# Wide gate and up products in four FFN parts, state space angle tables moved into the end of the second mix part, both score maps issued together

## The chip, the cores and the metric

The program runs on one core of one Trainium2 chip. The metric is the device time of one execution in microseconds (us). One execution was also profiled; all rows below are of that one.

## What is computed

The reference takes 256 tokens of width 1024 through three blocks. The first one has two layers; what matters of it:

```python
for l in range(DEPTH):                                   # 2 layers
    h = h + 0.5 * swiglu(rmsnorm(h, ffn1_norm[l]), ...)   # parts f10, f11
    u = rmsnorm(h, mix_norm[l])
    c_q, c_kv, k_rope, dq, dk, dv, p_in, z_gate = split(u @ w_in[l])
    # latent attention, differential attention (two softmax maps per head,
    # 8 heads), windowed pooling; each gated by sigmoid(z_gate) and projected
    h = h + merged @ w_out[l]                             # parts mx0, mx1
    h = h + 0.5 * swiglu(rmsnorm(h, ffn2_norm[l]), ...)   # parts f20, f21

swiglu(x) = (silu(x @ w_gate) * (x @ w_up)) @ w_down      # 1024 -> 2816 -> 1024
```

The second block (stick-breaking attention beside an S5 state space layer) and the third (gated linear attention) follow. For the S5 layer the kernel makes tables of sines and cosines of angles, from its parameters alone, some time before they are needed.

## The kernel before

**Numbers.** All products are float32 made of three matmuls on rounded parts: a weight tile `wh` (rounded) and `wl` (the rest), an activation tile hi and lo. `mm3` (L314) issues wh by hi, wh by lo, wl by hi into one accumulator: a *triple* (L317, L318, L319). Activations are held transposed, features on partitions and all 256 tokens (T) along the free axis, 8 chunks k for the width of 1024. Where tokens must stand on partitions (values, sigmoid gates), `tokens` multiplies the other way round, with 512 columns of the weight as the moving operand (L643 to L645).

**Weights.** `W()` (L299) takes the next weight piece, 128 x 1024, out of a raw buffer that SP's queue filled (two pieces a transfer, three buffers); ACT copies the rounded part `wh` (L311), DVE subtracts to get `wl` (L312). There are six wh/wl buffers: a piece takes the one of the piece six before it.

**FFN.** `ffn` (L532) runs over NF = 22 blocks f of 128 hidden features. For each: gate and up products by `project(f)` (two times 8 triples, gate and up being halves of one PSUM bank of tag a or b in turn), then the down products of block f-1 (8 triples into four banks of tag c, which stay open over the whole part), then the end of block f: DVE gate by the norm's row factor (L588), ACT silu (L589), POOL by half the row factor (L590), DVE by up (L591), `split` into hi on ACT (L339) and lo on DVE (L340). The result `hs[f]` is needed one block later, by down. Blocks 0 to 2 are projected early, while the norm's statistics are made. The last two blocks' down products stand at the end, bank by bank, so that the residual add of each bank can start.

**Mix.** `mix` (L717) makes latent attention, then differential attention in eight steps, one per head; `dscores` issues the score products of a head's two maps (32 rows of contraction each, one PSUM tile each) and their softmax. Between the steps stand fills for TensorE: the pooling windows (`window(g)`, on DVE), their products (`pooled(g)`, L848), value and gate projections and branch products. At the end of the part come the branch products with the differential output (`branch(1, g, ...)`, sinks L809 and L821 take them out of PSUM on ACT and DVE), the transposes of the differential output (`to_chunks`, L712; its scaling L933 on DVE), `turn(g)` (transposes of the merged output and its split, L339/L340), and the output projection (`out_steps`), whose results go to the next part's residual.

**S5 tables.** `s5_prep` (L959) returns a list of steps. `begin` makes step sizes and reduced angles with small operations on POOL, ACT and DVE that hand to one another (L979 to L991); eight `table` steps (two of 16 angle rows each) go DVE, POOL, DVE, POOL, POOL, DVE (L1001 to L1008); `sines` applies the sine on ACT; `begin_outs` to `direct` multiply out coefficient tables on POOL and DVE and transpose them. Part f21 takes one of these steps at the head of each block, f = 1 to 19.

**Order.** The program is written in the order of the parts. The tile framework then lists each engine's instructions by a scheduler that looks ahead; what an engine runs first is thus that list, and a wait holds all behind it on the same engine.

Of the kernel before, what the change touches and what calls it, by code (L numbers as in the profile page):

```python
# [238 lines left out]
class Kern:  # L239
# [75 lines left out]
    def mm3(self, ps, wh, wl, xh, xl, start, stop):  # L315
        mm = self.nc.tensor.matmul
        mm(ps, wh, xh, start=start, stop=False, skip_group_check=True)  # L317
        mm(ps, wh, xl, start=False, stop=False, skip_group_check=True)  # L318
        return mm(ps, wl, xh, start=False, stop=stop, skip_group_check=True)  # L319

    def proj(self, ps, w, xs, nk, off=0, m=P, stride=P):
        for k in range(nk):
            s = slice(off + k * stride, off + k * stride + m)
            last = self.mm3(ps, w[0][:, s], w[1][:, s], xs[0](k), xs[1](k), k == 0, k == nk - 1)
        return last

    def in_turn(self, pss, names, xs, starts):

        ws = [self.W(n) for n in names]
        for k in range(8):  # L330
            for ps, w, start in zip(pss, ws, starts):
                m = ps.shape[0]
                s = slice(k * m, k * m + m)
                self.mm3(ps, w[0][:, s], w[1][:, s], xs[0](k), xs[1](k), k == 0 and start, k == 7)
# [10 lines left out]
    def pair(self, n):  # L345

        s = [[self.slot(F32R) for _ in range((n + 3) // 4)] for _ in range(2)]
        return tuple((lambda k, q=q: q[k // 4][:, k % 4]) for q in s)
# [74 lines left out]
    def out_steps(self, tag, ks, ys, evac):  # L423
# [4 lines left out]
        def blk(w, k, d):  # L428
            self.mm3(acc[d // 2][:, (d % 2) * T:(d % 2) * T + T], w[0][:, d * P:(d + 1) * P],
                     w[1][:, d * P:(d + 1) * P], ys[0](ks[k]), ys[1](ks[k]),  # L430
# [101 lines left out]
    def ffn(self, part, l, h, extra=()):  # L532
# [6 lines left out]
        def down(f, d, w, hs):  # L539
            self.mm3(acc[d // 2][:, (d % 2) * T:(d % 2) * T + T], w[0][:, d * P:(d + 1) * P],  # L540
                     w[1][:, d * P:(d + 1) * P], hs[:, 0], hs[:, 1],
# [4 lines left out]
        def project(f, *ups):  # L546
            ups = ups or (0, 1)
            if f not in pgu:
# [8 lines left out]
            for k in range(8):  # L557
                for up, w in zip(ups, ws):
                    self.mm3(pgu[f][up], w[0][:, k * P:(k + 1) * P], w[1][:, k * P:(k + 1) * P],
                             xs[0](k), xs[1](k), k + up == 0, k == 7)  # L560

        for f in range(NF):
            if 0 < f <= len(extra):
                extra[f - 1]()
            if f == 0:
# [6 lines left out]
                with project(*todo.pop(0)):  # L572
                    stats(st[:, T:T + 2])
                project(*todo.pop(0))
                rb = self.rows(rc, st[:, 0:T])
                nc.scalar.activation(hrb, rb, AF.Copy, scale=0.5)
                project(*todo.pop(0))
            elif f == 1 and todo:
# [9 lines left out]
            nc.vector.tensor_tensor(gs, pg, rb, ALU.mult)  # L588
# [20 lines left out]
    def small_norm(self, cks, g, n):  # L609
# [18 lines left out]
        return (lambda k: hss[k][:, 0]), (lambda k: hss[k][:, 1])  # L628
# [88 lines left out]
    def mix(self, part, l, h):  # L717
# [143 lines left out]
        for f in more[1:] + gate(2, 0) + gate(2, 1) + branch(2, 0, yp) + branch(2, 1, yp) + \  # L861
# [32 lines left out]
        def dscores(hd):  # L894
# [3 lines left out]
            pp = []  # L898
            for m, rs in ((0, s0), (1, s1)):
# [752 lines left out]
```

## Time and profile before

| what | before |
|---|---|
| time, 3 runs | 1593.46, 1594.07 (median), 1594.55 us |
| the profiled execution | 1593.75 us |
| its span in the trace | 1592.0 us |
| TensorE busy | 1561.0 us, 98% of the span, 11662 matmuls |
| VectorE (DVE) busy | 1039.5 us, 65% |
| ScalarE (ACT) busy | 823.6 us, 52% |
| GpSimd (POOL) busy | 344.3 us, 22% |
| read from memory | 258.96 MB, 163 GB/s |

The time of an execution is its span plus some 1.8 us around it. A row of the timeline gives the start of an instruction, how long it took, engine, line, operation, output and inputs, and in brackets the idle time of the engine before it with what ended that. Matmuls overlap: how fast they follow one another is read from their starts, not from their lengths. A row with x4 stands for four instructions that follow one another, and its length is that of all four.

### The profile page before, as it was taken

The page shows a single profiled execution, that of the slowest core. Times are in us where ns is not written, and L with a number is a line of the kernel's source. Part 1 is how long each engine was busy: PE and PEld are TensorE (multiplying, and loading weights), DVE is VectorE, ACT ScalarE, POOL GpSimd, SP SyncE. Part 2 cuts the span into 40 slices and gives each one's busy share as a digit, 9 for nine tenths or more (in the row PEclk, how much of TensorE's full clock was granted, in tenths as well). Part 3 has the DMA queues.
Part 4 walks back from the last instruction along what each step waited for, and adds up shares of the span by engine and source line. Part 5 has one row for each costly group of instructions (what it writes and reads, how often), then busy time and mean ns, then how long its engine had stood idle before and what let it go on. Part 6 is the DMA issues. An engine that isn't in the chain of part 4 may idle for free.

```text
span 1592.0 us, 28666 instructions
## 1 busy us (share of the span) xinstructions
PE 1561.0 (98%) x11662; PEld 1451.4 (91%) x11662; DVE 1039.5 (65%) x1728; ACT 823.6 (52%) x1422; POOL 344.3 (22%) x414
## 2 busy tenths in 40 slices
PE   8999999999999999999999999999999999999998
PEld 8999998888999999999999878899899987899877
DVE  7655586575775557655576576776585787777743
ACT  6444455565454445444455556454444645566663
POOL 4111142001121112111132200244331321112232
PEclk9999999999999999999999999999999999999999
DMA  8555543344455554555544343554355443442430
GB/s 286 191 184 186 186 166 133 137 155 159 159 185 186 186 185 138 209 186 185 186 169 159 130 159 133 180 204 160 133 212 178 147 154 134 155 157 85 185 132 27
DMA packets 38451, 261.84 MB, mean 164 GB/s; under 512 B 4336, under 2 KB 5616, under 8 KB 7344
## 3 DMA queue, kind: packets, MB, share of 16 engines
q1 hardware_dynamic: 37440, 257.61, 45.0%
q0 software_dynamic: 736, 2.34, 0.5%
q8 instruction: 91, 1.49, 0.4%
q14 instruction: 40, 0.33, 0.1%
q10 hardware_dynamic: 144, 0.08, 0.0%
HBM read 258.96 MB, written 1.05 MB: 163 GB/s over the span
## 4 chain that ended last, share of the span: by engine, by line
PE 81%; DVE 8%; POOL 5%; ACT 3%; issue 3%; DMA 0%; SPq 0%; DVEq 0%; POOLq 0%; ACTq 0%
PE psa L318 7%; PE psa L317 7%; PE psa L319 7%; PE psc L318 6%; PE psc L319 6%; PE psc L317 6%; PE psb L317 5%; PE psb L318 5%; PE psb L319 5%; PE psa L643 5%; PE psa L645 5%; PE psa L644 5%; DVE wl L312 2%; ACT wh L311 1%; PE psb L643 1%
## 5 line engine op out<-in xcount | busy, mean ns | idle before, releaser
L312 DVE TENSOR_TENSOR wl<-raw,wh 128x1024 fp32r<-128x1024 f32 (+1 forms) x487 | 602.9, 1243 | 266.5 <-ACT wh L311 265.5
L311 ACT ACTIVATE wh<-raw 128x1024 fp32r<-128x1024 f32 (+1 forms) x487 | 507.8, 1050 | 417.9 <-PE psa L318 125.3
L317 PE MATMUL psa<-s,wh 128*128 128x256 f32 (+1 forms) x1224 | 349.3, 285 | 2.9 <-DVE s L1226 1.7
L318 PE MATMUL psa<-s,wh 128*128 128x256 f32 (+1 forms) x1224 | 348.4, 285 | 1.9 <-DVE s L343 1.5
L319 PE MATMUL psa<-s,wl 128*128 128x256 f32 (+1 forms) x1224 | 346.3, 283 | 0.2 <-DVE wl L312 0.2
L317 PEld LDWEIGHTS psa<-s,wh 128*128 128x128 f32 (+1 forms) x1224 | 233.7, 191 | 6.9 <-DVE s L1226 1.9
L318 PEld LDWEIGHTS psa<-s,wh 128*128 128x128 f32 (+1 forms) x1224 | 233.7, 191 | 6.1 <-DVE s L343 4.3
L590 POOL TENSOR_TENSOR t<-t,hrb 128x256 f32<-128x256 f32 x88 | 121.7, 1383 | 521.0 <-ACT t L589 521.0
L319 PEld LDWEIGHTS psa<-s,wl 128*128 128x128 f32 (+1 forms) x1224 | 233.8, 191 | 0.6 <-DVE wl L312 0.4
L319 PE MATMUL psb<-s,wl 128*128 128x256 f32 x752 | 212.9, 283 | 1.1 <-DVE wl L312 1.1
L317 PE MATMUL psb<-s,wh 128*128 128x256 f32 x752 | 213.6, 284 | 0.0
L318 PE MATMUL psb<-s,wh 128*128 128x256 f32 x752 | 212.8, 283 | 0.0
L317 PE MATMUL psc<-hs,wh 128*128 128x256 f32 x704 | 198.8, 285 | 4.5 <-ACT hs L339 4.5
L318 PE MATMUL psc<-hs,wh 128*128 128x256 f32 x704 | 200.3, 285 | 2.7 <-DVE hs L340 1.9
L319 PE MATMUL psc<-hs,wl 128*128 128x256 f32 x704 | 198.8, 283 | 0.0
L319 PEld LDWEIGHTS psb<-s,wl 128*128 128x128 f32 x752 | 144.3, 192 | 1.3 <-DVE wl L312 1.3
L317 PEld LDWEIGHTS psb<-s,wh 128*128 128x128 f32 x752 | 144.3, 192 | 0.5 <-ACT t L1335 0.3
L318 PEld LDWEIGHTS psb<-s,wh 128*128 128x128 f32 x752 | 144.4, 192 | 0.0
L317 PEld LDWEIGHTS psc<-hs,wh 128*128 128x128 f32 x704 | 134.3, 192 | 6.4 <-ACT hs L339 6.1
L318 PEld LDWEIGHTS psc<-hs,wh 128*128 128x128 f32 x704 | 135.0, 192 | 5.4 <-DVE hs L340 5.2
L643 PE MATMUL psa<-wh,s 128*128 128x512 f32 x336 | 137.5, 409 | 0.0
L319 PEld LDWEIGHTS psc<-hs,wl 128*128 128x128 f32 x704 | 135.1, 192 | 0.0
(390 smaller groups left out, 2514.6 us busy)
## 6 DMA issues: line engine op xcount, KB each, us to landing
raw<-in_w SPq DMA_DIRECT2D x242, 1024.0 KB, 4.8
s<-in_x SPq DMA_DIRECT2D x4, 256.0 KB, 5.4
raw<-in_w SPq DMA_DIRECT2D x4, 256.0 KB, 6.0
out<-t SPq DMA_DIRECT2D x8, 128.0 KB, 1.7
cst<-in_cst SPq DMA_DIRECT2D x1, 545.5 KB, 7.8
sq<-in_pw POOLq DMA_DIRECT2D x2, 256.0 KB, 3.7
s<-in_s5b POOLq DMA_DIRECT2D x1, 512.0 KB, 3.6
s<-in_s5c POOLq DMA_DIRECT2D x1, 512.0 KB, 3.7
```

The lines of the kernel that those rows point to most:

```text
L311: self.act = nc.scalar.activation(hi[:, s], src[:, s], AF.Copy)
L312: nc.vector.tensor_tensor(lo[:, s], src[:, s], hi[:, s].bitcast(F32), ALU.subtract)
L317: mm(ps, wh, xh, start=start, stop=False, skip_group_check=True)
L318: mm(ps, wh, xl, start=False, stop=False, skip_group_check=True)
L319: return mm(ps, wl, xh, start=False, stop=stop, skip_group_check=True)
L590: nc.gpsimd.tensor_tensor(sg, sg, hrb, ALU.mult)
L643: mm(ps[b], xs[0](k)[:, t], w[0][:, s], start=k == 0, stop=False, skip_group_check=True)
L644: mm(ps[b], xs[0](k)[:, t], w[1][:, s], start=False, stop=False, skip_group_check=True)
L645: mm(ps[b], xs[1](k)[:, t], w[0][:, s], start=False, stop=k == 2 * n - 1, skip_group_check=True)
```

## The change

1. `pair` now stores hi and lo of one chunk side by side, so that [hi | lo] is one operand of 512 columns. `mm3` and its callers take that pair; what they issue is as before.
2. A new function `wide` serves the gate and up products of blocks f = 3 to 21: in place of a triple it issues one matmul of wh by [hi | lo] (512 columns, into both halves of a bank) and one of wl by hi (256 columns, into the first half). Gate and up get a bank each, tags a and b. At the end of the block ACT copies the second half of each bank to a temporary and DVE adds the first half to it, for gate and for up (L611, L612); the rest of the chain (L613, L617, L618, L619, split L349 and L350) is as before.
3. The scores of a head's two maps are issued in turn: 128 columns of one and of the other, 256 columns of one and of the other. Both PSUM tiles are taken first.
4. `pooled(g)` stands one attention step later, two steps behind its window.
5. `begin` and the eight `table` steps are put in the second mix part's end, one behind each branch and output step; `sines`, cut in two, goes into block 0 of f21; the other S5 steps stand at f = 1 to 9 of f21.

```diff
-    def mm3(self, ps, wh, wl, xh, xl, start, stop):
+    def mm3(self, ps, wh, wl, x, start, stop):
...
+    def wide(self, ps, w, xs):
+
+        mm = self.nc.tensor.matmul
+        for k in range(8):
+            s = slice(k * P, k * P + P)
+            mm(ps, w[0][:, s], xs[2](k).rearrange("p a t -> p (a t)"), start=k == 0, stop=False,
+               skip_group_check=True)
+            last = mm(ps[:, 0:T], w[1][:, s], xs[0](k), start=False, stop=k == 7, skip_group_check=True)
+        return last
...
         def project(f, *ups):
             ups = ups or (0, 1)
+            if f > 2:
+                pgu[f] = self.psa("a"), self.psa("b")
+                for up in ups:
+                    last = self.wide(pgu[f][up], self.W(part + "gu"[up] + str(f)), xs)
+                return self.tc.issue_after(last.ins)
...
-            nc.vector.tensor_tensor(gs, pg, rb, ALU.mult)
+            if f > 2:
+                up = self.tmp()
+                for t, ps in ((gs, pg), (up, pu)):
+                    nc.scalar.activation(t, ps[:, T:2 * T], AF.Copy)
+                    nc.vector.tensor_tensor(t, ps[:, 0:T], t, ALU.add)
+                nc.vector.tensor_tensor(gs, gs, rb, ALU.mult)
+                pu = up
+            else:
+                nc.vector.tensor_tensor(gs, pg, rb, ALU.mult)
...
-            fills.append([lambda g=g: window(g)] if g == 0 else
-                         [lambda g=g: window(g), lambda g=g: pooled(g - 1)])
+            fills.append([lambda g=g: window(g)] if g < 2 else
+                         [lambda g=g: window(g), lambda g=g: pooled(g - 2)])
...
-        fills.append([more[0], lambda: pooled(3)])
+        fills.append([more[0], lambda: pooled(2)])
+        fills.append([more[1], lambda: pooled(3)])
...
-            pp = []
-            for m, rs in ((0, s0), (1, s1)):
-                i = 2 * hd + m
-                r = slice(32 * (i % 4), 32 * (i % 4) + 32)
-                ps = self.psa("b", 384)
-                self.qk(ps, dq[r, i // 4], dk[r, i // 4])
-                pp.append(self.softmax(ps, bias, [rs[:, hd:hd + 1], rs[:, 8 + hd:9 + hd]]))
+            pss = [self.psa("b", 384) for _ in range(2)]
+            rows = [slice(32 * (i % 4), 32 * (i % 4) + 32) for i in (2 * hd, 2 * hd + 1)]
+            for o, b, n in ((0, 0, P), (P, P, T)):
+                for r, ps in zip(rows, pss):
+                    nc.tensor.matmul(ps[:, o:o + n], dq[r, hd // 2, b:b + P], dk[r, hd // 2, 0:n],
+                                     start=True, stop=True)
...
         for g in range(2):
             for f in branch(1, g, yd, "ab"[g]):
                 f()
+                more()
...
+            prep = self.s5_prep() if l else ()
+            h = self.mix("mx%d" % l, l, h, prep[:9])
+            h = self.ffn("f2%d" % l, l, h, prep[11:], prep[9:11])
```

Where the instructions stand now. First ACT, in the end of the second mix part, around the two sinks of the last gate projection (`s<-psa,sm`: L809 before, L837 now; `sq` is the square sum of the differential output, `s5p` the S5 parameters, `vec` constants). Before:

```order
L921 ACTIVATE sq_11040<-psc_10354 128x512
L921 ACTIVATE sq_11043<-psc_10355 128x512
L311 ACTIVATE wh_11197<-raw_11195 128x1024
L809 ACTIVATE s_11084<-psa_10997,sm_9807 128x512
L809 ACTIVATE s_11084<-psa_10998,sm_9807 128x512
L311 ACTIVATE wh_11213<-raw_11195 128x1024
L311 ACTIVATE wh_11237<-raw_11235 128x1024
```

and with the change:

```order
L311 ACTIVATE wh_10628<-raw_10626 128x1024
L1020 ACTIVATE s5p_8620<-vec_86 128x16
L1023 ACTIVATE s5p_8620<-s5p_8620 128x16
L1024 ACTIVATE s5p_8620<-s5p_8620 128x16
L837 ACTIVATE s_10515<-psa_10428,sm_9238 128x512
L1030 ACTIVATE s5p_8620<-s5p_8620 128x16
L837 ACTIVATE s_10515<-psa_10429,sm_9238 128x512
L311 ACTIVATE wh_10665<-raw_10626 128x1024
L311 ACTIVATE wh_10703<-raw_10701 128x1024
```

Four operations of `begin` now stand between the weight copy and the two sinks, three ahead of the first and one between them.

Second DVE, a little later: the sinks of the branch products (L821 before, L849 now) and the scaling of the differential output (L933 before, L964 now; `t` are temporaries of the table steps). Before:

```order
L312 TENSOR_TENSOR wl_11214<-raw_11195,wh_11213 128x1024
L312 TENSOR_TENSOR wl_11238<-raw_11235,wh_11237 128x1024
L821 SCALAR_TENSOR_TENSOR s_10722<-s_10722,psa_11087 128x512
L821 SCALAR_TENSOR_TENSOR s_10722<-s_10722,psa_11088 128x512
L933 TENSOR_TENSOR s_11036<-psc_10354,sm_11038 128x512
L933 TENSOR_TENSOR s_11036<-psc_10355,sm_11038 128x512
```

and with the change:

```order
L312 TENSOR_TENSOR wl_10666<-raw_10626,wh_10665 128x1024
L1046 TENSOR_SCALAR t_10686<-t_10686 128x256
L1041 TENSOR_SCALAR t_10720<-cst_85,s5p_8620 128x128
L1040 TENSOR_SCALAR t_10754<-cst_85,s5p_8620 128x128
L1041 TENSOR_SCALAR t_10755<-cst_85,s5p_8620 128x128
L1043 TENSOR_SCALAR t_10721<-t_10721 128x256
L1040 TENSOR_SCALAR t_10754<-cst_85,s5p_8620 128x128
L312 TENSOR_TENSOR wl_10704<-raw_10701,wh_10703 128x1024
L849 SCALAR_TENSOR_TENSOR s_10153<-s_10153,psa_10518 128x512
L849 SCALAR_TENSOR_TENSOR s_10153<-s_10153,psa_10519 128x512
L964 TENSOR_TENSOR s_10467<-psc_9785,sm_10469 128x512
L964 TENSOR_TENSOR s_10467<-psc_9786,sm_10469 128x512
```

Between the weights' second parts and the sinks now stand six table operations, among them L1046 and L1043, each of which takes what POOL made of the operations before.

Third ACT at the end of an FFN part (f10), from the weight ahead of block 21's gate to the rounding of its result. Before:

```order
L311 ACTIVATE wh_2425<-raw_2419 128x1024
L311 ACTIVATE wh_2486<-raw_2484 128x1024
L589 ACTIVATE t_2266<-t_2265 128x256
L339 ACTIVATE hs_2272<-t_2267 128x256
L311 ACTIVATE wh_2520<-raw_2484 128x1024
```

and with the change:

```order
L611 ACTIVATE t_2070<-psa_2026 128x256
L311 ACTIVATE wh_2296<-raw_2294 128x1024
L611 ACTIVATE t_2073<-psb_2027 128x256
L617 ACTIVATE t_2071<-t_2070 128x256
L311 ACTIVATE wh_2330<-raw_2294 128x1024
L349 ACTIVATE hs_2082<-t_2072 128x256
```

The two copies of the second halves are new, and a weight copy of the next part stands between them, another one ahead of the rounding L349.

## Rows read from the trace of the kernel before

**Rows 1.** Page, part 1: busy time, share of the span and instructions of each engine.

```profile
PE 1561.0 (98%) x11662; PEld 1451.4 (91%) x11662; DVE 1039.5 (65%) x1728; ACT 823.6 (52%) x1422; POOL 344.3 (22%) x414
```

**Rows 2.** Timeline of PE in f10; 57 matmuls of 256 columns, first and last.

```profile
99.73 0.28 PE L319 MATMUL psa<-s,wl 128*128 128x256 f32 x1
...
106.45 0.28 PE L318 MATMUL psb<-s,wh 128*128 128x256 f32 x1
```

**Rows 3.** Timeline of PE in the first mix part; 24 matmuls of 512 columns, first and last.

```profile
389.65 0.39 PE L645 MATMUL psa<-wh,s 128*128 128x512 f32 x1
...
394.86 0.40 PE L645 MATMUL psb<-wh,s 128*128 128x512 f32 x1
```

**Rows 4.** Timeline of PE in the second mix part; 6 matmuls of 512 columns, first and last.

```profile
1005.00 0.40 PE L644 MATMUL psa<-wl,s 128*128 128x512 f32 x1
...
1006.17 0.39 PE L643 MATMUL psa<-wh,s 128*128 128x512 f32 x1
```

**Rows 5.** Timeline of PE, the scores of one head's two maps (two records a matmul).

```profile
346.23 0.50 PE L664 MATMUL psb<-s 32*128 32x128 f32 x4
346.55 0.60 PE L665 MATMUL psb<-s 32*128 32x256 f32 x4
```

**Rows 6.** Groups by line and form: pooling products; busy, mean ns | idle before, releaser.

```profile
L848 PE MATMUL psc<-t,sq 128*128 128x256 f32 x16 | 5.3, 411 | 3.1 <-DVE t L842 3.1
```

**Rows 7.** Groups by line and form: weights' two parts and the end of an FFN block.

```profile
L312 DVE TENSOR_TENSOR wl<-raw,wh 128x1024 fp32r<-128x1024 f32 x482 | 599.9, 1250 | 265.0 <-ACT wh L311 264.0
L311 ACT ACTIVATE wh<-raw 128x1024 fp32r<-128x1024 f32 x482 | 505.0, 1055 | 415.8 <-PE psa L318 125.3 <-PE psb L318 91.0 <-PE psa L645 72.5
L590 POOL TENSOR_TENSOR t<-t,hrb 128x256 f32<-128x256 f32 x88 | 121.7, 1383 | 521.0 <-ACT t L589 521.0
L588 DVE TENSOR_TENSOR t<-psb,rb 128x256 f32<-128x256 f32 x44 | 18.6, 423 | 18.1 <-PE psb L319 18.1
L339 ACT ACTIVATE s<-psa 128x256 fp32r<-128x256 f32 x16 | 5.4, 378 | 3.7 <-DVE s L340 3.7
```

**Rows 8.** Timeline of PE at the end of f10, first products of the last hidden block.

```profile
197.81 0.38 PE L317 MATMUL psc<-hs,wh 128*128 128x256 f32 x1 [0.25 <-ACT hs L339]
198.27 0.39 PE L318 MATMUL psc<-hs,wh 128*128 128x256 f32 x1
```

**Rows 9.** Timeline of PE: starts of like matmuls in f20 (two) and f21 (three).

```profile
437.29 0.28 PE L317 MATMUL psa<-s,wh 128*128 128x256 f32 x1
468.76 0.28 PE L317 MATMUL psa<-s,wh 128*128 128x256 f32 x1
...
1054.96 0.28 PE L317 MATMUL psa<-s,wh 128*128 128x256 f32 x1
1087.99 0.28 PE L317 MATMUL psa<-s,wh 128*128 128x256 f32 x1
...
1182.73 0.28 PE L317 MATMUL psa<-s,wh 128*128 128x256 f32 x1
```

**Rows 10.** Groups by line and form: the last step of a table but one, on DVE.

```profile
L1007 DVE TENSOR_SCALAR t<-t 128x256 f32<-128x256 f32 x8 | 2.9, 360 | 13.0 <-POOL t L1006 13.0
```

**Rows 11.** Timeline of all engines in the second mix part's end.

```profile
1002.66 2.93 POOL L927 TENSOR_TENSOR sm<-sm,cst 128x16 f32<-128x16 f32 x1 [110.49 <-DVE sm L926]
1003.92 1.37 ACT L809 ACTIVATE s<-psa,sm 128x512 f32<-128x512 f32 x2 [0.98 <-PE psa L645]
1004.67 0.50 PE L643 MATMUL psa<-wh,s 128*128 128x512 f32 x1
1011.17 1.28 DVE L933 TENSOR_TENSOR s<-psc,sm 128x512 f32<-128x512 f32 x2
1012.76 0.49 PE L712 MATMUL psc<-cst,s 128*128 128x128 f32 x3
1029.44 0.75 DVE L340 TENSOR_TENSOR s<-psa,s 128x256 fp32r<-128x256 f32 x2
1029.91 0.39 PE L318 MATMUL psc<-s,wh 128*128 128x256 f32 x1 [0.25 <-DVE s L340]
```

More of the change, by code (lines that the diff above doesn't have):

```diff
@@ L333, in in_turn @@
                 s = slice(k * m, k * m + m)
-                self.mm3(ps, w[0][:, s], w[1][:, s], xs[0](k), xs[1](k), k == 0 and start, k == 7)
+                self.mm3(ps, w[0][:, s], w[1][:, s], xs[2](k), k == 0 and start, k == 7)
     def split(self, hi, lo, src, scale=None):
@@ L345, in pair @@
     def pair(self, n):
-        s = [[self.slot(F32R) for _ in range((n + 3) // 4)] for _ in range(2)]
-        return tuple((lambda k, q=q: q[k // 4][:, k % 4]) for q in s)
+        s = [self.slot(F32R) for _ in range((n + 1) // 2)]
+        return ((lambda k: s[k // 2][:, k % 2 * 2]), (lambda k: s[k // 2][:, k % 2 * 2 + 1]),
+                (lambda k: s[k // 2][:, k % 2 * 2:k % 2 * 2 + 2]))
     def chunks(self, n=8):
@@ L530, in reduce_angle, with ffn @@
         eng.tensor_scalar(y, y, PI, -PI, ALU.min, ALU.max)
-    def ffn(self, part, l, h, extra=()):
+    def ffn(self, part, l, h, extra=(), early=()):
         nc = self.nc
@@ L715, in to_chunks, with mix @@
                 self.split(ys[0](2 * c2 + j), ys[1](2 * c2 + j), ps[:, j * T:(j + 1) * T], scale)
-    def mix(self, part, l, h):
+    def mix(self, part, l, h, extra=()):
         nc = self.nc
@@ L855, in mix @@
         for g in range(4):
-            fills.append([lambda g=g: window(g)] if g == 0 else
-                         [lambda g=g: window(g), lambda g=g: pooled(g - 1)])
+            fills.append([lambda g=g: window(g)] if g < 2 else
+                         [lambda g=g: window(g), lambda g=g: pooled(g - 2)])
         more = self.tokens([part + "dv%d" % i for i in range(4)], xs,
                            lambda b, ps: nc.scalar.activation(dv[:, b], ps, AF.Copy, scale=rc[:, b:b + 1]))
-        fills.append([more[0], lambda: pooled(3)])
-        for f in more[1:] + gate(2, 0) + gate(2, 1) + branch(2, 0, yp) + branch(2, 1, yp) + \
+        fills.append([more[0], lambda: pooled(2)])
+        fills.append([more[1], lambda: pooled(3)])
+        for f in more[2:] + gate(2, 0) + gate(2, 1) + branch(2, 0, yp) + branch(2, 1, yp) + \
                 gate(0, 0) + gate(0, 1) + gate(1, 0) + gate(1, 1):
@@ L941, in mix, with more @@
         ms = self.pair(8)
+        extra = list(extra)[::-1]
+        def more():
+            if extra:
+                extra.pop()()
         for g in range(2):
@@ L956, in mix @@
                 turn(1)
+            more()
         return hn
@@ L1010, in table, with turn, sines2 @@
                 self.abs = nc.scalar.activation(view(tabs[-1], 1), view(tabs[-1], 0), AF.Abs)
+        def turn(ts):
+            for t in ts:
+                sn, cs = view(t, 0), view(t, 1)
+                nc.scalar.activation(sn, sn, AF.Sin)
+                nc.scalar.activation(cs, cs, AF.Sin, bias=self.c("hpi"), scale=-1.0)
+        def sines2():
+            with self.tc.issue_after(self.act.ins):
+                turn(tabs[2:])
         def sines():
-            with self.tc.issue_after(self.abs.ins):
+            with self.tc.issue_after(self.act.ins):
                 nc.scalar.activation(sb, y, AF.Sin)
@@ L1394, in even @@
             nc.vector.scalar_tensor_tensor(h(k), h(k), self.v("final_norm", k), rfb, ALU.mult, ALU.mult)
-        ys = [lambda k, j=j: ysa[k // 4][j](k % 4) if k < 8 else ysb[j](k - 8) for j in range(2)]
+        ys = [lambda k, j=j: ysa[k // 4][j](k % 4) if k < 8 else ysb[j](k - 8) for j in range(3)]
         steps = self.out_steps("eo", [8, 9, 10, 11, 0, 1, 2, 3, 4, 5, 6, 7], ys,
```

35 lines of the change are left out of this document (18 added, 17 removed).

## Prediction

> **What bounds the kernel now.** First the busy shares: TensorE works 1561.0 of 1592.0 us [rows 1], every other engine two thirds or less. So a change counts only as far as it shortens the stream of matmuls or takes away, or makes, one of the pauses in it, some 31 us in all. Then the timeline of PE, for the distance from one start to the next: matmul lengths overlap and tell nothing. 56 steps between matmuls of 256 columns take 106.45 - 99.73 = 6.72 us, 0.120 each [rows 2]; 23 steps of 512 columns take 5.21, 0.2265 each [rows 3]. So 512 columns cost less than twice 256. Then the groups and the timeline around the pauses: who ended each one, and what stood ahead of that on its engine.
>
> The sum is made against the profiled execution, 1593.75 us; the median of the three runs is 1594.07, so it stands 0.3 below.
>
> **1. Wide products.** A triple is three steps of 0.120, 0.360 us; the new form is one step of 512 and one of 256 columns, 0.2265 + 0.120 = 0.3465. That saves 13.5 ns, and I count 13. There are 4 parts x 19 blocks x 2 products x 8 chunks = 1216 of them: **-15.8 us**. Bounds: directly behind a wait, five steps of 512 columns took 1.17 us, 0.234 each [rows 4], which leaves 6 ns, counted down to 5: -6.1. At best 15 ns, -18. I take the long undisturbed run of rows 3, since gate and up products form just such runs. The rows are read as a fixed cost of 13 ns for each matmul. The Trainium skill (TensorE: Matmul & The Clock Gate, "Back-to-back issue gap") gives the warm distance as columns by 2.4 plus 2.5 ns. By it a triple would save only 2.5 ns, 3.0 us in all; the measured 120 ns against its 109 for 256 columns speaks against it here.
>
> The block's end grows. Per block DVE gets three wl at 1.25 and five operations near 0.42, 5.9 us; ACT three wh at 1.06 and four operations near 0.38, 4.7 us; POOL keeps 1.38 [rows 7]. A block takes PE 24 x 0.120 + 16 x 0.3465 = 8.4 us, so all three fit beside it. The chain behind the last up product: ACT copy 0.38, DVE add 0.42, then multiply, hi and lo, with the gate's silu and POOL beside the up product at best. With everything in line (three ACT 0.38, four DVE 0.42, POOL 1.38, one wh 1.06 and one wl 1.25 ahead) it is 6.5 us, and its result is wanted one block later: 1.9 us of cover. **0**; the case without cover is rival C. Two PSUM banks for each block instead of one leave each tag's second buffer for the next block: 0.
>
> **2. Ends of the FFN parts.** The last block's products have no later block as cover: PE stopped 0.25 for hi [rows 8], then 0.46 - 0.12 = 0.34 for lo, 0.6 us, four times, 2.4. The gate now has its own bank, so silu starts while up is still multiplied; against that, weight copies stand between the two copies and ahead of hi, as the order of ACT shows. **-2.0**; bounds 0 (the weight copy takes the gain back) to -2.4.
>
> **3. Scores of two maps.** The program of before issues 128 and 256 columns of one map and then of the other. The trace has four records of 128 columns together and then four of 256 [rows 5]: two maps of two records each, already side by side. **0**. The Trainium skill (TensorE: Matmul & The Clock Gate, "What overlaps and what doesn't" in Part 3) says that matmuls keep strictly to program order. By that the old order would have run one map behind the other, and the new one would bring them together; rows 5 speak against it (rival E).
>
> **4. Pooling one step later.** Its 16 matmuls waited 3.1 us in all for DVE's window [rows 6]. With a whole attention step between, the window is long done: **-3.1**; bounds 0 to -3.1. It takes the place of other fill work of the same length, so what follows keeps its cover.
>
> **5. S5 steps out of f21.** The first two blocks of f21 took 1087.99 - 1054.96 = 33.03 us, f20's 468.76 - 437.29 = 31.47: 1.56 more. The next ten took 94.74; undisturbed they take ten times 72 steps of 0.120, 86.40: 8.34 more [rows 9]. Together 9.9. What leaves: `begin` and the tables, whose steps change three times between DVE and POOL and hold DVE for 13.0 us in all [rows 10]. What stays: sines in the first block, which need ACT before the norm's squares, and nine coefficient steps that now begin at block 1, ahead of the silu chain. I leave the start its 1.56 and those steps 2.6 (some third of 8.34): **-5.7**. Bounds -2 (the coefficient steps disturb the first blocks as much as all did) to -8.
>
> **6. The same steps in the second mix part's end.** Three places, each where a queue now waits for POOL ahead of something that PE needs.
> - ACT: the gate sinks ran at 1003.92, and PE took the bank freed by the first at 1004.67 [rows 11], with nothing to spare. Now three small operations stand ahead, of which L1023 (lines here are those of the changed program) waits for a product on POOL. POOL was in a power from 1002.66 to 1005.59 just then [rows 11]; with 0.7 for the product and two short ACT operations (an estimate) the sink starts near 6.27 instead of 3.92: 2.35. The second sink waits for L1030, at the end of the angle reduction (POOL, DVE, POOL), another 1.0 (an estimate): 3.4.
> - DVE: the differential output's scaling ran at 1011.17 to 1012.45, PE wanted it at 1012.76 [rows 11], 0.3 later. Six table operations now stand ahead, one with the wait of rows 10, 13.0 / 8 = 1.6: 1.6 + 0.9 - 0.3 = 2.2.
> - The split of the merged output: lo at 1029.44, PE already stopped 0.25 for it [rows 11]. One table's wait, 1.6, and two operations: 2.1.
>
> Sum **+7.7**. Bounds +3 (ACT's stop alone) to +13 (all of rows 10's wait lands on PE). The middle, because DVE has the tables at three places out of eight ahead of something urgent. No new work on SP's queue: the three constant loads of `begin` are issued by POOL, ahead of its arithmetic, and land long before the coefficient steps.
>
> Sum: -15.8 - 2.0 + 0 - 3.1 - 5.7 + 7.7 = **-18.9**. 1593.75 - 18.9 = 1574.85; I say **1575**.
>
> **The rivals.**
> - A: the mix part's end is covered. The scheduler's list is what ACT and DVE run, but the tables may slip into idle time: ACT was busy about half of that stretch. Against it: the sinks stand behind them by order, and PE's bank came just in time [rows 11]. Then 7.7 goes: 1567.
> - B: the wide form saves 5 ns [rows 4]: 1593.75 - 6.1 - 3.1 = 1584.6. For it: the steps behind a wait. Against it: rows 3. By the page's rule the wide form would give 3.0, so 1587.7; 0.02 of this rival's chance is for it.
> - C, slower: the block's chain is longer than a block. If two wh and two wl stand in line with it, it is 2 x 1.06 + 3 x 0.38 + 4 x 0.42 + 1.38 + 2 x 1.25 = 8.8 us [rows 7], 0.4 above 8.4, in each of 76 blocks: 30 us, 1605. It decides as soon as the chain passes 8.4. For it: DVE and ACT lists have weights between all steps. Against it: 1.9 us of cover, and weight copies wait for a free buffer, so they rarely are ready at the worst moment.
> - D: DVE bounds the mix part's end; all of the waits for POOL, 13.0 [rows 10] plus 1.9 for the shorter ones (an estimate), and ACT's 3.4 reach PE: 18.3 in place of 7.7, so 1585.5.
> - E: the scores were one behind the other. Then some 0.9 us a head (0.32 between the first starts, then up to 0.60 [rows 5]) times 16 heads, 14 us more is won: 1561. Rows 5 show the contrary.
>
> **How the numbers follow.** Forecast 0.55, A 0.13, B 0.14, D 0.10, C 0.06, E 0.01, 0.01 for anything else. The predicted time is the likeliest case, 1575. Its own terms move it by some 6 either way. The range takes in A below, B and D above: 1564 to 1588; C and E lie outside. A measurement of this kernel can tell about 0.2%, 3.2 us, from no change. Faster by more: all but C and bad mixtures of B and D, 0.90. Within: B together with D, 0.04. Slower: 0.06.
>
> **What would show it.** Wide products 0.3465 us apart pair by pair in f10, and 16.85 us for two undisturbed blocks (144 steps of 0.120 less 32 x 0.0135); at 17.1 it is B. No wait of `down` in the middle of a part (C). The pooling group without idle time. PE idle before a branch product that waits for ACT's sinks, before the transposes of the differential output, and ahead of the output projection, each of some 2 to 3 us (A: none). In f21 ten blocks behind the first two within 3 us of an undisturbed stretch. I am wrong if the four FFN parts together lose less than 10 us, or if the mix part's end grows by more than 13.

## The result and the profile after

The changed kernel takes 1603.99 us (median of 4 runs, 1602.95 to 1606.02) against 1594.06: a ratio of 1.0064, 95% interval 1.0052 to 1.0076. The forecast was 1575 within 1564 to 1588. It became slower by 10 us where 19 less were expected. The time comes out near rival C's 1605, but that is chance: C's mechanism is not what happened.

The page of the changed kernel, busy time by engine, and the view by cores:

```profile
PE 1558.9 (97%) x10446; PEld 1395.4 (87%) x10446; DVE 1090.6 (68%) x1880; ACT 865.6 (54%) x1575; POOL 330.8 (21%) x414
```

```profile
core 0: 1601.2 us, clock 0.989
```

Against [rows 1] the stream has 1216 matmuls less, yet PE's busy time fell by 2.1 us only. The same view of the kernel before reads 1592.0 us and 0.999. The clock has two levels, 2.4 and 1.2 GHz; a mean of 0.989 means half clock in 0.011 / 0.5 = 2.2% of the span, some 35 us, against 3 before. No term of the prediction had that.

Where the time went is best seen by cutting the program at the first and last down products of the FFN parts (their starts in PE's timeline; the last row ends at the start of the last matmul). All numbers are us; "wide alone", "scores, pooling" and "S5 move too" (scores, pooling and the S5 move, with triples) are experiments told below, and the last column is the best version found.

| stretch | before | changed | wide alone | scores, pooling | S5 move too | best |
|---|---|---|---|---|---|---|
| start to f10's first down | 29.78 | 30.41 | 29.82 | 29.92 | 30.08 | 30.11 |
| down products of f10 | 173.39 | 170.96 | 170.95 | 173.40 | 173.39 | 169.33 |
| first mix part | 251.16 | 252.08 | 252.83 | 250.54 | 250.60 | 250.50 |
| down products of f20 and f11 | 366.50 | 361.61 | 361.84 | 366.49 | 366.45 | 358.23 |
| second mix part | 252.76 | 271.28 | 255.64 | 251.99 | 265.73 | 253.48 |
| down products of f21 | 184.01 | 177.78 | 183.94 | 183.92 | 179.47 | 173.46 |
| all behind | 330.27 | 333.04 | 334.50 | 330.47 | 331.21 | 331.44 |

So the FFN parts did win, f10 2.4, f20 with f11 4.9 and f21 6.2 us, and one stretch ate it all: the second mix part, 18.5 us longer.

**Wide products.** PE's timeline in f10, one block's gate and up products of the changed kernel, 16 pairs; the row at 110.16 is the first matmul behind them:

```profile
104.50 0.40 PE L326 MATMUL psa<-s,wh 128*128 128x512 f32 x1
104.74 0.28 PE L328 MATMUL psa<-s,wl 128*128 128x256 f32 x1
104.86 0.40 PE L326 MATMUL psa<-s,wh 128*128 128x512 f32 x1
...
110.16 0.28 PE L317 MATMUL psc<-hs,wh 128*128 128x256 f32 x1
```

The 16 pairs take 5.65 us, 353 ns each: 0.24 us behind the wide matmul and 0.12 behind the narrow one. Triples take 360 ns [rows 2], and 346.5 was forecast from [rows 3]. The 0.234 of the steps directly behind a wait [rows 4], which was meant as the low bound, comes near what the pairs show all along.

**The second mix part's end.** All of PE's pauses with a releaser between 1002 and 1044 in the changed kernel (first of the two sinks' banks, second, the transposes of the differential output, the output projection's hi and lo):

```profile
1004.93 0.50 PE L671 MATMUL psa<-wh,s 128*128 128x512 f32 x1 [1.89 <-ACT s L837]
1006.54 0.50 PE L671 MATMUL psa<-wh,s 128*128 128x512 f32 x1 [0.64 <-ACT s L837]
1017.07 0.30 PE L740 MATMUL psc<-cst,s 128*128 128x128 f32 x1 [2.99 <-DVE s L964]
1017.58 0.98 PE L740 MATMUL psc<-cst,s 128*128 128x128 f32 x7 [0.21 <-DVE s L964]
1038.43 0.81 PE L317 MATMUL psc<-s,wh 128*128 128x256 f32 x4 [3.69 <-ACT s L349]
1040.74 0.58 PE L318 MATMUL psc<-s,wh 128*128 128x256 f32 x1 [1.50 <-DVE s L350]
```

These are the three places of the prediction. ACT's is smaller (2.5 us against 3.4), the other two are larger (3.2 against 2.2 at the transposes; 5.2 at the output projection, of which a wait of 0.61 for hi and of 0.25 for lo [rows 11] stood there before, against 2.1 more). The kernel before has, from 985 to 1050, this one beside the row of [rows 11]:

```profile
1028.93 0.73 PE L317 MATMUL psc<-s,wh 128*128 128x256 f32 x4 [0.61 <-ACT s L339]
```

**The clock behind a pause.** The same kernel, behind f11: PE's timeline shows the pause before the norm's statistics and what follows it.

```profile
824.20 1.01 PE L391 MATMUL psc<-cst,t 128*128 128x1 f32 x4 [2.38 <-POOL t L411]
825.08 0.56 PE L318 MATMUL psb<-s,wh 128*128 128x256 f32 x1
825.43 0.41 PE L319 MATMUL psb<-s,wl 128*128 128x256 f32 x1
825.65 0.41 PE L317 MATMUL psb<-s,wh 128*128 128x256 f32 x1
```

Matmuls of 256 columns now start 0.21 us apart instead of 0.12. The stretches of that place and of the output projection (columns: stretch and its length; PE, weight loads, DVE, ACT, POOL busy; then the granted clock):

```profile
820.00:824.00 4.00, 1.82 (x16) 1.62 (x14) 3.39 (x2) 3.10 (x4) 3.77 (x3) 0.99 0.27 61
824.00:828.00 4.00, 3.80 (x18) 3.80 (x19) 2.43 (x3) 0.00 (x0) 1.77 (x2) 0.50 0.66 223
...
1036.00:1040.00 4.00, 0.81 (x4) 0.54 (x4) 4.00 (x10) 2.12 (x4) 2.19 (x3) 0.87 0.00 0
1040.00:1044.00 4.00, 3.26 (x15) 3.26 (x16) 3.42 (x9) 0.72 (x2) 1.64 (x1) 0.50 0.00 0
```

PE is idle for half of a stretch or more, and the next one runs at half clock. Summing, over all matmuls that start at half clock, what their spacing exceeds that at full clock gives some 12 to 14 us in the changed kernel (by how the matmuls beside a wait are counted) and 1.4 in the one before. A pause can thus cost twice: the time that PE waits, and the slower matmuls behind it.

### The profile page after: what moved, and what is told of

Read it like the earlier page. It is cut to its first block, busy times and chain, and to the rows that moved or that the text cites. A ratio compares the mean times of both kernels' runs of the same rounds, so it can differ in the third digit from the quotient of the medians.

```text
span 1601.2 us, 26661 instructions
## 1 busy us (share of the span) xinstructions
PE 1558.9 (97%) x10446; PEld 1395.4 (87%) x10446; DVE 1090.6 (68%) x1880; ACT 865.6 (54%) x1575; POOL 330.8 (21%) x414
## 4 chain that ended last, share of the span: by engine, by line
PE 85%; DVE 6%; POOL 4%; ACT 3%; issue 1%; DMA 0%; SPq 0%; POOLq 0%; DVEq 0%; ACTq 0%
PE psb L326 9%; PE psa L326 9%; PE psc L318 7%; PE psc L317 7%; PE psc L319 7%; PE psa L671 5%; PE psb L328 5%; PE psa L328 4%; PE psa L673 4%; PE psa L672 4%; PE psa L318 4%; PE psa L317 4%; PE psa L319 4%; DVE wl L312 2%; PE psb L671 1%
## 5 line engine op out<-in xcount | busy, mean ns | idle before, releaser
L618 POOL TENSOR_TENSOR t<-t,hrb 128x256 f32<-128x256 f32 x88 | 103.9, 1181 | 578.3 <-ACT t L617 554.0
L326 PE MATMUL psa<-s,wh 128*128 128x512 f32 x608 | 219.0, 399 | 0.1
L326 PE MATMUL psb<-s,wh 128*128 128x512 f32 x608 | 218.0, 398 | 0.0
L317 PE MATMUL psa<-s,wh 128*128 128x256 f32 (+1 forms) x648 | 187.2, 290 | 3.4 <-DVE s L1272 1.7
L318 PE MATMUL psa<-s,wh 128*128 128x256 f32 (+1 forms) x648 | 186.4, 288 | 2.3 <-DVE s L353 2.1
L319 PE MATMUL psa<-s,wl 128*128 128x256 f32 (+1 forms) x648 | 184.9, 286 | 0.2 <-DVE wl L312 0.2
L328 PE MATMUL psa<-s,wl 128*128 128x256 f32 x608 | 171.1, 281 | 0.0
L671 PE MATMUL psa<-wh,s 128*128 128x512 f32 x336 | 137.9, 410 | 2.5 <-ACT s L837 2.5
L326 PEld LDWEIGHTS psb<-s,wh 128*128 128x128 f32 x608 | 114.2, 188 | 28.4
L326 PEld LDWEIGHTS psa<-s,wh 128*128 128x128 f32 x608 | 114.7, 189 | 24.9 <-DVE t L619 0.4
L673 PE MATMUL psa<-wh,s 128*128 128x512 f32 x336 | 132.1, 393 | 0.0
L672 PE MATMUL psa<-wl,s 128*128 128x512 f32 x336 | 131.9, 392 | 0.0
L317 PEld LDWEIGHTS psa<-s,wh 128*128 128x128 f32 (+1 forms) x648 | 124.6, 193 | 7.4 <-DVE s L1272 1.9
```

The source lines that it names most:

```text
L317: mm(ps, wh, x[:, 0], start=start, stop=False, skip_group_check=True)
L318: mm(ps, wh, x[:, 1], start=False, stop=False, skip_group_check=True)
L319: return mm(ps, wl, x[:, 0], start=False, stop=stop, skip_group_check=True)
L326: mm(ps, w[0][:, s], xs[2](k).rearrange("p a t -> p (a t)"), start=k == 0, stop=False, skip_group_check=True)
L328: last = mm(ps[:, 0:T], w[1][:, s], xs[0](k), start=False, stop=k == 7, skip_group_check=True)
L618: nc.gpsimd.tensor_tensor(sg, sg, hrb, ALU.mult)
```

## The experiments

**The parts of the change.** Four kernels each take something out. First the S5 steps back in f21:

```diff
-            h = self.mix("mx%d" % l, l, h, prep[:9])
-            h = self.ffn("f2%d" % l, l, h, prep[11:], prep[9:11])
+            h = self.mix("mx%d" % l, l, h, ())
+            h = self.ffn("f2%d" % l, l, h, prep)
```

> The changed kernel with the S5 steps back in f21's blocks 1 to 19, all else as changed. Theory 1 (the S5 steps in the second mix part's end cost the time, by PE pauses of some 11 us and by the half clock that follows them): the mix part from the last down product of f11 to the first of f21 falls from 271.3 us to about 253, f21 gives back some 4, so 1588 to 1590. Theory 2 (the wide products and their longer block end cost the time): 1600 or more.

Measured 1594.41 (ratio to before 1.0006, 0.9997 to 1.0016). The second mix part's loss is gone (253.70 us), but the total stays 5 above the expectation: wide products with a mix part left in peace win nothing. Theory 1 holds for the S5 move, and something of theory 2 is true as well.

Second, triples in place of the wide products, all else changed (`f > 2` becomes never, in `project` and in the block's end):

> The changed kernel with gate and up products as triples again; the S5 move, pooling one step later and scores together stay. Theory 1: the S5 move costs 10 to 16 by itself, so 1604 to 1610. Theory 2: near 1594, or below it by the few us that f21 wins.

Measured 1604.31 (1.0065, 1.0050 to 1.0080), as theory 1 had it. Third, the wide products alone:

> The kernel before with the wide products alone. By the spacing in the changed kernel's trace, 236 + 117 = 353 ns a pair instead of 360, 1216 pairs win 8.5 us; the norm's statistics behind two FFN parts come later and cost some 2.5 each. Theory 1: 1588 to 1592. Theory 2: 1600 or more. With the 13.5 ns of the prediction it would be below 1582.

Measured 1595.18 (1.0010, 1.0001 to 1.0019), 3 above theory 1 and below theory 2. The table shows how: 7.1 us won in the down stretches of f10, f20 and f11, nothing in f21, 4.6 lost in the two mix parts' stretches, 4.2 behind f21. In f21 the block's longer end meets the S5 steps; PE's timeline of this kernel has, in five blocks one behind the other (1100 to 1139), a row like

```profile
1110.05 0.39 PE L318 MATMUL psc<-hs,wh 128*128 128x256 f32 x1 [0.81 <-DVE hs L350]
```

The waits of the down products of f21 come to 7.2 us here, against 5.1 in the kernel before, and a stretch of half clock stands at 1161 us.

Fourth, only the scores and the pooling:

> The kernel before with only the pooling one step later and the scores of two maps together. Theory: the waits before the pooling products turn up again before the transposes of the softmax (four pauses of 0.8 to 1.2 us in the changed kernel's trace), so 1594 within 1. Rival (the prediction's term): 3.1 us less, 1591. If the old scores had run one map behind the other: 1580.

Measured 1592.83 (0.9995, 0.9985 to 1.0004): no difference that can be told. The groups by line and form say why, first the softmax's transposes in the kernel before, then these and the pooling products in the changed kernel (and, with the same numbers, in this one):

```profile
L671 PE MATMUL psc<-cst,t 128*128 128x128 f32 x96 | 15.7, 272 | 0.0
```

```profile
L699 PE MATMUL psc<-cst,t 128*128 128x128 f32 x96 | 15.9, 274 | 3.4 <-DVE t L878 3.4
L876 PE MATMUL psc<-t,sq 128*128 128x256 f32 x16 | 4.8, 378 | 0.0
```

The pooling products, 3.1 us idle before [rows 6], wait no more, but the transposes of the softmax behind them do, 3.4 us for L878, the operation by which DVE takes a pooling product out of its PSUM bank. The late work was on DVE's queue, and PE meets it one step further on.

**The spacing of pairs.** The same wide products, in another order within a product:

```diff
         for k in range(8):
             s = slice(k * P, k * P + P)
             mm(ps, w[0][:, s], xs[2](k).rearrange("p a t -> p (a t)"), start=k == 0, stop=False,
                skip_group_check=True)
+        for k in range(8):
+            s = slice(k * P, k * P + P)
             last = mm(ps[:, 0:T], w[1][:, s], xs[0](k), start=False, stop=k == 7, skip_group_check=True)
```

> The kernel before with the wide products alone, but each product issues its eight 512-column matmuls first and then its eight 256-column ones. If the change between widths or weights costs the missing 6 ns a pair, like matmuls in a row stand 0.2265 and 0.120 apart again: 7.9 us less than with pairs in turn, so about 1587. If the 512-column form of this operand costs it by itself (236 ns), nothing changes: 1595.

Measured 1582.69 (0.9931, 0.9916 to 0.9946), 12.5 below pairs in turn. PE's timeline, the start of the 16 pairs and the first matmul behind:

```profile
103.78 1.09 PE L326 MATMUL psa<-s,wh 128*128 128x512 f32 x4
...
109.36 0.28 PE L317 MATMUL psc<-hs,wh 128*128 128x256 f32 x1
```

5.59 us against 5.65, 349 ns a pair. That is 76 x 0.063 = 4.8 us over the program. The rest is pauses and the clock: by the cuts of the table this kernel's profile is 5.2 us shorter in the down stretches of f10, f20 and f11, 4.7 in the two mix parts' stretches (the pauses there are told next) and 3.9 behind f21, but 2.8 longer in f21, where the waits are as long as with pairs in turn (7.1 us) and the clock is at half for 10 us instead of 3. Then two and two in turn, both loops inside one over pairs of chunks:

```diff
+        for k2 in range(0, 8, 2):
+            for k in (k2, k2 + 1):
...
+            for k in (k2, k2 + 1):
```

> The kernel before with the wide products alone, two 512-column matmuls and then two of 256 in turn: half as many changes of width as with pairs. If each change of width costs, 16 pairs take half way between 5.650 (in turn) and 5.587 (in a row), 5.62 us. If only the first few of a product cost, or the order of the operands in memory, 5.65 or 5.59.

Measured 1591.19 (0.9982, 0.9971 to 0.9992). PE's timeline:

```profile
104.13 0.63 PE L327 MATMUL psa<-s,wh 128*128 128x512 f32 x2
104.60 0.39 PE L331 MATMUL psa<-s,wl 128*128 128x256 f32 x2
...
109.70 0.28 PE L317 MATMUL psc<-hs,wh 128*128 128x256 f32 x1
```

5.57 us: less than eight in a row, not half way. So it is not each change of width that costs, nor the operand, which is the same in all three. The strict turn of one and one is slower than the two other orders; why stays open. The total is 8.5 above eight in a row all the same, for this kernel has the pauses of 2.38 us behind f10 and f11, told next, and eight in a row has not. How the whole of the 8.5 divides was not taken apart.

**The ends of the FFN parts.** Triples in the last three blocks of each part (`2 < f < 19`), wide alone:

> The kernel before with the wide products in blocks 3 to 18 only, triples in the last three blocks of each part. If the later end of the FFN parts (the pause before the norm's statistics and the clock behind it) eats the gain, the two mix parts start as before: 3 to 5 us less than with all 19 blocks wide, less 1.3 of gain given up: 1591 to 1593. If it is not the ends: 1596.

Measured 1589.69 (0.9971, 0.9961 to 0.9981), 5.5 below all 19 blocks wide, with fewer wide pairs. What ends late is the norm's sum of squares. POOL's timeline behind f11 in the changed kernel, then behind f10 in the kernel with like widths in a row:

```profile
814.19 1.80 POOL L411 TENSOR_TENSOR t<-t 128x256 f32<-128x256 f32 x2 [4.88 <-ACT t L409]
818.10 6.05 POOL L411 TENSOR_TENSOR t<-t 128x256 f32<-128x256 f32 x5 [2.12 <-ACT t L409]
```

```profile
197.72 2.59 POOL L413 TENSOR_TENSOR t<-t 128x256 f32<-128x256 f32 x3 [4.35 <-ACT t L411]
202.30 3.39 POOL L413 TENSOR_TENSOR t<-t 128x256 f32<-128x256 f32 x4 [2.00 <-ACT t L411]
```

The first follows ACT's list, which has three squares (L409) ahead of the eight roundings (L352) and five behind:

```profile
813.38 1.08 ACT L409 ACTIVATE t<-s 128x256 f32<-128x256 f32 x3 [2.77 <-DVE s L634]
814.37 3.29 ACT L352 ACTIVATE s<-s,vec 128x256 fp32r<-128x256 f32 x8
817.57 1.63 ACT L409 ACTIVATE t<-s 128x256 f32<-128x256 f32 x5
```

So five additions at 1.2 us each run at the end, and PE stops 2.4 us. In the second there are four and four, the additions take 0.85, and PE does not stop. Nothing in the source says so: the scheduler made another list once the products were issued in another order, and behind f10 and f11 the pairs in turn, one and one or two and two, got the bad one. In the changed kernel the pause was the same at both places, but the clock fell behind f11 only; behind f10 the matmuls at once stand 0.12 apart. It is not the place that decides: in the kernel with the S5 steps back in f21 (`no_s5`) the pause is 2.37 us at both places, and there the clock fell behind f10 and not behind f11:

```profile
212.00:216.00 4.00, 4.00 (x27) 4.00 (x27) 2.05 (x3) 1.00 (x2) 1.07 (x1) 0.73 0.82 291
828.00:832.00 4.00, 4.00 (x36) 4.00 (x36) 3.33 (x6) 1.38 (x2) 0.69 (x2) 1.00 0.69 254
```

**The S5 move, taken apart.** All with triples, pooling and scores as changed, so to be held against 1592.83 without the move and 1604.31 with it. Only `begin` in the mix part's end (`prep[:1]`); the other S5 steps stay in f21 as before:

> Pooling and scores as changed, triples, and of the S5 steps only begin in the second mix part's end; tables, sines and the rest in f21. Theory: ACT's two pauses before the gate sinks (2.5 us) stay, the two others (3 before the transposes of the differential output, 5 before the output projection) go: 1595 to 1596. If begin starts the rest by its delay: 1600 or more. If the tables alone cost: 1593.

Measured 1596.55 (1.0017, 1.0007 to 1.0026): ACT's two pauses, 2.5 us, and a stretch of half clock behind them; f21, at 183.95 us, gains nothing. Then all of the move again, with `begin` issued earlier, ahead of the last gate projections (the table steps behind it then move up by one place each):

```diff
+        extra = list(extra)[::-1]
+        if extra:
+            extra.pop()()
         fill(len(fills))
...
-        extra = list(extra)[::-1]
```

> Triples, pooling and scores as changed, tables in the second mix part's end, but begin is issued ahead of the last gate projections, where POOL has been idle. If ACT's two pauses (1.9 and 0.6) came from begin standing behind POOL's power, they go, and the pauses before the transposes and the output projection stay: 1601 to 1602 against 1604.3. If the tables then only move up and fill the gap with new waits: 1604.

Measured 1603.83 (1.0066, 1.0052 to 1.0079). Its pauses before the gate sinks, 2.3 us without the early `begin`, are gone, but the one before the transposes has grown from 1.7 to 7.6:

```profile
1019.64 2.26 PE L740 MATMUL psc<-cst,s 128*128 128x128 f32 x8 [7.62 <-DVE s L967]
```

Then the tables without POOL:

```diff
-            g.tensor_tensor(w, u, v, ALU.add)
+            nc.vector.tensor_tensor(w, u, v, ALU.add)
...
-            g.tensor_tensor(u, u, w, ALU.subtract)
-            g.tensor_tensor(u, u, v, ALU.add)
+            nc.vector.tensor_tensor(u, u, w, ALU.subtract)
+            nc.vector.tensor_tensor(u, u, v, ALU.add)
```

> As triples with the S5 move, but the three POOL operations of each table step run on DVE, so no table operation waits for POOL. If the queue's waits for POOL delay the transposes and the output projection, their pauses shrink from 3 and 5 us to under half: 1597 to 1600 against 1604.3. If it is DVE's own work standing ahead (three more operations of 0.4 a step now), 1604 or more.

Measured 1597.14 (1.0020, 1.0011 to 1.0029): more work on DVE, and 7.2 us less. The groups by line and form on DVE from 1004 to 1050 with the tables shared with POOL, then with the tables on DVE alone:

```profile
L312 DVE TENSOR_TENSOR wl<-raw,wh 128x1024 fp32r<-128x1024 f32 x8 | 11.9, 1488 | 0.0
L1040 DVE TENSOR_SCALAR t<-cst,s5p 128x128 f32<-128x128 f32 x16 | 7.5, 466 | 1.5 <-POOL s5p L1027 1.5
L1041 DVE TENSOR_SCALAR t<-cst,s5p 128x128 f32<-128x128 f32 x16 | 6.9, 434 | 0.1
...
L1046 DVE TENSOR_SCALAR t<-t 128x256 f32<-128x256 f32 x7 | 2.2, 314 | 1.4 <-POOL t L1045 1.4
L1043 DVE TENSOR_SCALAR t<-t 128x256 f32<-128x256 f32 x7 | 2.0, 288 | 1.9 <-POOL t L1042 1.9
```

```profile
L312 DVE TENSOR_TENSOR wl<-raw,wh 128x1024 fp32r<-128x1024 f32 x8 | 9.8, 1220 | 0.0
L1041 DVE TENSOR_SCALAR t<-cst,s5p 128x128 f32<-128x128 f32 x14 | 4.7, 332 | 0.1
L1040 DVE TENSOR_SCALAR t<-cst,s5p 128x128 f32<-128x128 f32 x14 | 3.9, 281 | 1.5 <-POOL s5p L1027 1.5
```

POOL cost DVE in two ways. It made it wait (1.4 and 1.9 us for tables), and it made DVE's own operations longer: on average `wl` 1.49 instead of 1.22 us, L1040 0.47 instead of 0.28, L1041 0.43 instead of 0.33. Over these 40 instructions that is 8 x 0.27 + 16 x 0.19 + 16 x 0.10 = 6.8 us, twice the waits. The averages hide how it happens. The timeline of the kernel that shares the tables with POOL shows two meetings of the engines:

```profile
1025.27 2.15 POOL L850 TENSOR_TENSOR s<-s 128x512 f32<-128x512 f32 x1
1026.19 1.31 DVE L1040 TENSOR_SCALAR t<-cst,s5p 128x128 f32<-128x128 f32 x1
```

```profile
1009.97 1.85 POOL L1044 TENSOR_TENSOR t<-t 128x256 f32<-128x256 f32 x1 [0.41 <-DVE t L1043]
1010.00 1.22 DVE L312 TENSOR_TENSOR wl<-raw,wh 128x1024 fp32r<-128x1024 f32 x1
```

In the first DVE begins while POOL works, and L1040 ends just behind POOL's operation, after 1.31 us instead of 0.28. In the second they begin 0.03 apart; DVE keeps its 1.22, and POOL's operation takes 1.85 where it takes 0.74 at 1028.52. Where the two meet, one of them waits for the other. Over the whole trace of this kernel, 442 `wl` began while POOL was idle, and none took over 1.23 us; 45 began while POOL was at work, and 23 of them took over 1.3, up to 2.30. Operations of DVE that read PSUM, like L849, kept their 0.67 beside POOL. The stretch of 28 us in three kernels, without the move, with it, and with the tables on DVE (columns as above):

```profile
1004.00:1032.00 28.00, 27.16 (x142) 22.83 (x141) 22.62 (x31) 12.96 (x19) 6.47 (x5) 1.00 0.46 155
```

```profile
1012.00:1040.00 28.00, 21.73 (x98) 16.71 (x97) 26.69 (x50) 10.68 (x15) 19.17 (x20) 0.95 0.46 169
```

```profile
1012.00:1040.00 28.00, 24.21 (x120) 20.36 (x119) 28.00 (x62) 11.84 (x17) 6.76 (x7) 0.94 0.45 166
```

DVE had 5.4 us free there without the move; with it DVE is nearly or wholly full, and PE falls from 27.2 to 21.7. That DVE is the bound there is read from this and from what the tables' move to DVE won.

**Putting it together.** Three versions with like widths in a row. The changed kernel with that alone:

> The changed kernel whole, only with like widths in a row within each product. If the turn of widths cost there what it cost with the wide products alone (12.5 us, of which 4.8 by the spacing and the rest by the pauses at the ends of f10 and f11 and the clock behind them), then 1604 - 12 = 1592; if only the spacing, 1599.

Measured 1587.59 (0.9961, 0.9947 to 0.9974), 4 better than the better of the two expectations. With the tables on DVE as well:

> The changed kernel with like widths in a row and the table steps on DVE alone. If the two causes are separate, their gains add: 1587.6 less the 7.2 that the table steps on DVE won among triples, 1580 to 1581, level with the version that keeps the S5 steps in f21. If DVE is full now that the wide blocks load it more, 1585 or more.

Measured 1582.73 (0.9929, 0.9914 to 0.9944): 4.9 less than without it, not 7.2, so the gains add in part. With `begin` early as well:

> The same with begin ahead of the last gate projections. The early begin won nothing while tables waited for POOL, because they filled the gap (a pause of 7.6 us before the transposes). If that pause was their wait for POOL, the two pauses before the gate sinks go for good: 1578. If DVE's own table work takes the place again: 1581 or more.

Measured 1572.79 (0.9868, 0.9852 to 0.9885), 21.3 us below the kernel before and the best of all. PE's pauses with a releaser from 985 to 1045 are two:

```profile
1015.70 0.74 PE L317 MATMUL psc<-s,wh 128*128 128x256 f32 x4 [0.61 <-ACT s L351]
1018.42 0.39 PE L318 MATMUL psc<-s,wh 128*128 128x256 f32 x1 [1.98 <-DVE s L352]
```

and the view by cores shows the clock back:

```profile
core 0: 1570.6 us, clock 0.999
```

So the same early `begin` that won nothing among triples while the tables used POOL wins 9.9 us here, where they do not; that it is POOL's share of the tables and not the wide products that makes the difference was not run by itself. The two versions that keep the S5 steps in f21 do less well. Triples in f21 and in the last three blocks of the other parts:

> A version meant to beat both: pooling and scores as changed, S5 steps in f21 as before, wide products with like widths in a row in blocks 3 to 18 of f10, f20 and f11, triples elsewhere. 768 pairs: 10 us less if like widths in a row give 13 ns, 5 if 7 ns, so 1583 or 1588 against 1592.8 with pooling and scores alone.

Measured 1584.84 (0.9943, 0.9928 to 0.9958). Triples in f21 only:

> The version meant to beat both: pooling and scores as changed, S5 steps in f21 as before, wide products with like widths in a row in all blocks from 3 on of f10, f20 and f11, triples in f21. Measured so far: 16 pairs take 5.587 us in a row, 5.650 in turn, 5.760 as triples. 912 pairs by 10.8 ns are 9.9 us: 1583, or about 1581 if the ends of the parts are as short as with like widths in a row in all parts; 1585 or more if the last three blocks are better left as triples.

Measured 1581.57 (0.9927, 0.9914 to 0.9941).

## Why the prediction was wrong

The sum missed at several terms, and none of them alone turns it. The largest are the first, the second and the sixth, 6 to 7 us each.

**1, wide products: wrong by half.** The term -15.8 was 1216 x 13 ns; the pairs win 6.9 ns (5.65 us for 16 pairs against 5.76), -8.4. The step that failed is the choice of [rows 3]: runs of matmuls all of 512 columns, read as a fixed cost for each matmul, carried over to 512 and 256 in turn. Rival B named the nearer row [rows 4], whose 6 ns (counted as 5) come close to the 6.9, and had 1584.6 for it. The rule of the Trainium skill cited there (TensorE: Matmul & The Clock Gate, "Back-to-back issue gap"), which the section gives for a matmul by itself and not for a stream, would have left 2.5 ns; the trace shows 6.9, and 10.8 in a row, so it does not price this stream either.

The block's end cost nothing in f10, f20 and f11, as forecast: no down product waited over 0.25 us there in the changed kernel, so rival C's chain was never the bound. In f21 it was, beside the S5 steps: wide alone gained nothing in f21's stretch.

**2, ends of FFN parts: wrong sign.** Forecast -2.0; the kernel with the wide products alone loses 1.7 and 2.9 in the stretches behind f10 and f11. The step that failed is the path: the pauses for hi and lo [rows 8] did go, but the norm's statistics became late by a pause of 2.38 us at each place, with half clock behind the second. I had costed the last block's chain and not what stands behind it in ACT's and POOL's lists.

**3, scores: right.** No difference, by [rows 5]; rival E's 14 us are refuted by the 1592.83 of scores and pooling together. The scores were not run alone.

**4, pooling: wrong.** Forecast -3.1; the wait moved to the next matmul that needs a bank of the same kind, where 3.4 us stand. "The window is long done" was true, and the pooling group stands without idle time, as was named for a sign; but the operation behind the product on DVE's queue was not counted. Pooling and scores together come out 1.0 us lower, and the interval takes in no difference.

**5, S5 steps out of f21: right within its bounds.** Forecast -5.7; 183.92 to 179.47, -4.5.

**6, the mix part's end: right places, too small.** Forecast +7.7, at most 13; 251.99 to 265.73 with triples, +13.7, some 3 of it at half clock. ACT's stop was 2.5 against 3.4. The step that failed is the price of the other two places, one table's wait for POOL each, 1.6 [rows 10]: what was missing is that DVE had only 5.4 us of 28 free, and that an operation of DVE that begins beside one of POOL takes longer. The runs show both: tables on DVE alone win 7.2. That is rival D's name, DVE as the bound, though its price (18.3, from waits) came from elsewhere. On this the Trainium skill has a line (GPSIMD Engine Reference, "Specifications"): POOL shares its SBUF interfaces with VectorE, with contention where a DVE instruction has two SBUF inputs or a two-port mode. The trace agrees for `wl`, which reads two tiles, 1.49 against 1.22 us on average. I had not drawn on it.

**7, missing from the sum: the clock.** Some 12 to 14 us are lost at half clock against 1.4. Much of it lies inside the stretches above: behind the pauses of the mix part's end, behind f11's statistics, and in the part after f21. That pauses bring it is inferred: in every trace PE stood idle for some 0.7 us or more shortly before each such stretch, it is nearly gone (0.999) in the best version, where the pauses are short, and no run sets the clock by itself. Nor does a pause decide alone, as f10 and f11 show.

Put together: -8.4 for pairs, +4.6 at two part ends, +13.7 and -4.5 for the S5 move, all from single kernels, and +2.8 behind f21 and +0.6 at the start, from the changed kernel itself, make +8.8; the profiled spans differ by 9.2. That it comes so close is partly chance: pooling's up to 1.0, the pairs of f21 that won nothing by themselves (2.1), and what the parts do to one another are not in it.

## What to carry to other kernels

Before work is moved into a stretch, read how much of each engine is free there (the windows), not only who waits for whom: DVE, 81% busy, was full once POOL worked beside it. Price a pause of TensorE at its length and, as the worse case, slower matmuls behind it. And price a new order of matmuls by a row of that very order, since one and one, two and two, eight and eight of the same instructions took between 5.57 and 5.65 us. Where a scheduler makes the lists, read the new list behind the place that was changed, too.

## What was not expected of the hardware

- 16 pairs of 512 and 256 columns take 5.65 us in turn, 5.59 in a row of eight each, and 5.57 two and two.
- The half clock followed a pause of PE of 2.4 us behind f11 (spacing 0.21 us instead of 0.12), but the same pause behind f10 left it at full; in another kernel with the same two pauses it was the other way round.
- Where operations of DVE and POOL met, one of them was held up: L1040 on DVE, 0.28 us otherwise, took 1.31 when it began while POOL was at work, and POOL's L1044 took 1.85 instead of 0.74 beside a `wl`. L1040 reads one tile and a column of scalars.
